# Gate rows of the forgetting attention: one load per pair, copied on ScalarE, triangle added on VectorE

## The chip, the cores and the metric

The kernel runs on one core of a Trainium2 chip. Its time is the device time of one execution in microseconds, and the time before is the median of three runs: 617.68 us (615.83, 617.68, 619.33).

## What is computed

The block normalises 512 tokens and 16 learned meta tokens ahead of them (L = 528, width 1024) and projects them with one combined weight into everything that follows. There are two attentions of 16 heads each: latent attention (MLA, with low-rank queries and keys and a rotary part) and forgetting attention (FoX, in the code's names `fox`). Both are causal; the second adds the cumulative log forget gate `cum` to its scores. Each output is gated by `silu` of a projection `z`, projected, mixed by two sigmoids, projected again, normalised and added to the input.

```
q (B,H,L,64), k, v:  s = q k^T * scale
fox only:            s = s + (cum[t] - cum[s])
s = where(key_pos <= query_pos, s, -inf);  p = softmax(s);  o = p v
y = (o * silu(z)) @ W_branch
h = h + rmsnorm_post((sigmoid(ga) * y_mla + sigmoid(gb) * y_fox) @ W_out)
```

In a row of the softmax the term `cum[t]` is the same for all keys and drops out, so that only the key's `cum[s]` has to be added: one row of 528 numbers for each head, the same for every query.

## The kernel before

**Stages.** A stage is one branch and one pair of heads, written (1,pr) for fox and (0,pr) for latent, pr = 0 to 7, in the order (1,0), (0,0), (1,1), (0,1) and so on. Each stage makes the scores of its pair for the four blocks of 128 queries (`s0` blocks 0 to 2, `s1` block 3), takes exponents on ScalarE (ACT; `e0`, `e1`), normalises them into probabilities `pn` in two float16 halves, high on ACT and low on VectorE (DVE; `n0`, `n1`), has the DMA engines transpose them into `pt`, and multiplies with the values (`va`, tile `ov`), which is done within the next stage.

**Fill.** Between these parts TensorE (PE) does the projections that later stages need, as a list of steps called `fill`. In a fox stage it is: 8 steps `za` (fox's own `z`), the transposes `vt` of the own values, `mq` (latent query), and then `mk` (latent keys, 2 steps), `v` (latent values, 2 steps) between the 8 steps of `zb` (the latent `z`). In a latent stage it is the next pair's `fq`, `vt`, `fk`, `v`. Products are three-pass: each operand stands as a high and a low part. A weight arrives as `wraw` by DMA, ACT casts its high part `wh`, and DVE or GpSimd (POOL) makes the remainder `wl` (helper at L117). Query and key go the same way into `hlq` and `hlk`: high part by ACT (L266), low part by DVE (L117), both from PSUM. The banks of these accumulators are few: the second key product takes the bank of `mq`, the first value product that of the first key product, so each waits until DVE has read the earlier one.

**The gate's rows.** `cdiag` [128, 2, 528] holds the two `cum` rows of a pair on all 128 partitions, loaded by `load_diag` (L285, two loads). `mask_diag` (L295) adds the causal triangle `maskt` to its four diagonal blocks. Blocks left of the diagonal need the rows without a triangle: `load_off` (L289) loads the first 400 numbers of each once more, into a free part of `gT`, two loads a pair. `terms` hands the scores the one or the other and L927 on DVE adds them as it reads the score from PSUM. Pair 0 is prepared at the start, where DVE adds the triangle; for pairs 1 to 7 POOL does.

**What sets the order.** Up to the end of stage (1,0) the order on all engines is written out by hand (lists of names, and the branch `si == 0`). In later stages only PE's order is by hand; on the other engines, SyncE (SP) with its DMA queue included, a scheduler places an instruction by its priority and by when its inputs and its buffer are free. So the rows of pair pr + 1 are loaded in stage (1,pr), once the scores of pair pr no longer read `cdiag`, though the code issues them with the keys in stage (0,pr). Each engine works its instructions in order, so an instruction that waits holds all behind it.

Of the kernel before, what the change touches and what calls it, by code (L numbers as in the profile page):

```python
# [17 lines left out]
ALU = mybir.AluOpType  # L18
# [8 lines left out]
NH = 16  # L27
KD = D // 128
# [26 lines left out]
def block_kernel(ctx: ExitStack, tc: tile.TileContext, x, meta_tokens, pre_norm_g, w_in, fox_forget_b,  # L55
                 mla_q_norm_g, mla_kv_norm_g, w_uq, w_ukv, w_br_mla, w_br_fox, w_out, post_norm_g,
                 rope_tok, rope_pe, out):
    nc = tc.nc
# [25 lines left out]
    c_dram = dram.tile([NH, L], F32, tag="cdram", name="c_dram")  # L84
# [16 lines left out]
    def total(cols):  # L101

        ps = acc(f"sum{uid[0]}")[:, 0:1]
        uid[0] += 1
        for i, c in enumerate(cols):
            mm(ps, ALL1, c, start=(i == 0), stop=(i == len(cols) - 1))
        return ps
# [85 lines left out]
    def unit(name, getw, act, nk, sls, done):  # L193

        st = {}
        out = []

        def make(eng=None, later=None):
            if "w" not in st:
                st["w"] = getw(eng, later) if eng else getw()  # L200
                loads = getattr(out[0][1], "nxt", ())
                if later is None:
                    for load in loads:
                        load()
                else:
                    later.extend(loads)

        for i, sl in enumerate(sls):
            n = sl.stop - sl.start
            for k in range(nk):  # L210
                def fn(i=i, sl=sl, k=k, n=n):
                    make()
                    if k == 0:
                        st["ps"] = acc(f"{name}{i}")
                    ps = st["ps"][:, :n]
                    (wh, wl), (ah, al) = st["w"], act(k)
                    for q, (w, a) in enumerate(((wh, ah), (wh, al), (wl, ah))):
                        mm(ps, w(k), a[:, sl], start=(k == 0 and q == 0), stop=(k == nk - 1 and q == 2))
                    if k == nk - 1:
                        done(i, ps)  # L220
                out.append((3 * n / 2.4, fn))
        out[0][1].make = make
        if hasattr(getw, "load"):
            out[0][1].load = getw.load
        return out
# [13 lines left out]
    def win_w(off, i):  # L239
        return weights(lambda: [win[:, :, off + 128 * i : off + 128 * i + 128]], lambda w: by_k(w[0], KD))  # L240

    def run(steps):
        for _, fn in steps:
            fn()
# [6 lines left out]
    cdiag = fx.tile([128, 2, L], F32, tag="cdiag", name="cdiag")  # L251
# [3 lines left out]
    def hl_done(key, n, w, put=None):  # L255

        def done(i, ps):
            if i == 0:
                hls[key] = hlp.tile([128, 2, n], F32R, tag=f"hl{key[0]}", name="hl" + "".join(map(str, key)))
            hl = hls[key]  # L260
            o = w * i
            w_ = min(w, n - o)

            def upper():
                with tc.high_priority(offset=30):
                    nc.scalar.copy(hl[:, 0, o : o + w_], ps)  # L266

            def lower():
                with tc.high_priority(offset=30):
                    split_lo(nc.vector, hl[:, 1, o : o + w_], ps, hl[:, 0, o : o + w_])  # L270
            if put:
                put(i, upper, lower)
            else:
                upper()
                lower()
        return done
# [4 lines left out]
    OFF = META + 384  # L281

    def load_diag(pr):
        for h in range(2):
            nc.sync.dma_start(cdiag[:, h], c_dram[2 * pr + h : 2 * pr + h + 1, :].broadcast_to([128, L]))  # L285

    def load_off(pr):
        for h in range(2):
            nc.sync.dma_start(gT[h][:, KD - 1, 0:OFF],  # L289
                              c_dram[2 * pr + h : 2 * pr + h + 1, 0:OFF].broadcast_to([128, OFF]))  # L290

    def mask_diag(eng):
        d = cdiag[:, :, META:].rearrange("p h (b c) -> p h b c", b=4)
        m = maskt[:, 400:L].unsqueeze(1).unsqueeze(1).broadcast_to([128, 2, 4, 128])
        eng.tensor_tensor(out=d, in0=d, in1=m, op=ALU.add)  # L295

    def k_fox(pr, put=None):
        halves = hl_done(("k", 1, pr), L, HALF, put)

        def done(i, ps):  # L300
            halves(i, ps)
            if pr > 1 and i:
                load_diag(pr)
                load_off(pr)
                mask_diag(nc.gpsimd)
        return unit(f"fk{pr}", win_w(O_FK, pr), u_act, KD, ALLT, done)


# [63 lines left out]
    def lo(name):  # L372

        def fn():
            for f in lows[name]:
                f()
        return fn
# [292 lines left out]
    with ExitStack() as att:  # L670
# [327 lines left out]
        vts = {}  # L998

        def feed(br, pr):  # L1000

            q = (q_mla, q_fox)[br](pr)
            k = (k_mla, k_fox)[br](pr)
            v, vts[br, pr] = v_unit(br, pr, put=(br, pr) == (0, 0))
            return q, k, v
# [8 lines left out]
        for si, (br, pr) in enumerate(stages):  # L1014
            last = si + 1 == len(stages)
            if not last:
                q, k, v = feed(*stages[si + 1])
            if br == 1:

                za, zb = z_unit(1, pr), z_unit(0, pr)  # L1020
                fill = za + vts[br, pr] + q + zb[:4] + k + zb[4:6] + v + zb[6:]
            elif not last:
                fill = q[:3] + vts[br, pr] + q[3:] + k + v
            else:
                g = gate_unit()
                g2 = gate_unit()

                def g_scale():
                    pow2_scale(sg[1], isg[1], total([gss[:, 1, c : c + 1] for c in range(4)]))
                fill = g[:4] + vts[br, pr] + g[4:] + g2[:4] + [(100, g_scale)] + g2[4:]  # L1030
            if si == 0:
                early = za[0][1], q[0][1], zb[0][1]
            fills.append(fill)
# [3 lines left out]
        za, q, zb = early  # L1037
# [10 lines left out]
        with tc.manual_schedule(engines={E_.PE, E_.SP, E_.Pool, E_.Activation, E_.DVE}):  # L1048
            for name in MIDDLE:
                later[name]()  # L1050
            lctx.close()
            gT = [gctx[b].enter_context(tc.tile_pool(name=f"gp{b}", bufs=1, side="right")).tile(
                [128, KD, S], F32, tag=f"gT{b}", name=f"gT{b}") for b in range(2)]
            later.update(r1=lambda: rope0[1](1), r0=lambda: rope0[1](0), Lf=fills[1][0][1].load,
                         Lo=lambda: load_off(0), bt=lambda: mask_diag(nc.vector))
            for name in LAST:
                later[name]()
        pe, pe_turn, pe_rest, _ = pe_unit(1)
# [5 lines left out]
        for si, (br, pr) in enumerate(stages):  # L1064
            (s0, e0), (s1, e1), n0, n1, va = attention(br, pr)

            fill = fills[si]
            with ExitStack() as head:
                if si == 0:
                    head.enter_context(tc.manual_schedule(engines={E_.PE, E_.SP, E_.Pool, E_.Activation, E_.DVE}))  # L1070
                    s0()
                    e0()
                    run(fill[:3])
                    lo("b")()
                    nxt[1].load()
                    nxt[2].load()
                    n0()
                    s1()
                    run(fill[3:9])
                    e1()  # L1080
                    run(fill[9:11])
                    n1()
                    load_diag(1)
                    load_off(1)
                    for x in (1, 0):
                        for i in range(2):
                            rope0[2](i, x, 2)
                    run(fill[11:17])
                    nxt[0].make()
                    run(fill[17:21])  # L1090
                    for name in ("vr0", "vr1", "vs", "vz"):
                        later[name]()
                    nxt[1].make()
                    run(fill[21:])
                    later["vT"]()
                    nxt[2].make()
                    mask_diag(nc.gpsimd)
                else:
                    s0()
                    e0()  # L1100
                    for fn in late:
                        fn()
                    s1()
                    e1()
                    run(fill[:4])
                    n0()
                    run(fill[4:11])
                    n1()
                    run(fill[11:])
            late = [va]  # L1110
# [281 lines left out]
    with rctx, ExitStack() as og:  # L1392
# [38 lines left out]
        for t in range(4):  # L1431
# [12 lines left out]
            for m in range(2):  # L1444
                sm = slice(512 * m, 512 * m + 512)
                nc.vector.scalar_tensor_tensor(out=yo[:, t, sm], in0=yo[:, t, sm], scalar=ss[:, t, 3:4],
                                               in1=xr[:, t, sm], op0=ALU.mult, op1=ALU.add)
# [44 lines left out]
```

## Time and profile before

| | us |
|---|---|
| median of three runs | 617.68 |
| profiled execution, its own time | 620.4 |
| its span | 618.4 |
| PE busy | 601.8 |
| DVE busy | 400.9 |
| ACT busy | 384.0 |
| POOL busy | 192.9 |
| first value product of (0,0) | 111.83 |

Rows of a timeline give start, duration, engine, line, operation, output and inputs, shape and count; in brackets stands the idle time before it and what ended that. Where a row counts several instructions, the duration is that of all. A row of windows gives, per engine in the order PE, PE's weight load, DVE, ACT, POOL, the busy time, then PE's granted clock as a share of the full one, the share of DMA and GB/s. A row of the waits view gives: engine, what waited, for what, us in total, times, longest. The shares of busy time are means over stages that differ.

### The profile page before, as it was taken

To read this page: it belongs to the slowest core of one execution; us is meant where nothing else is said; L and a number is where in the kernel's file an instruction comes from. 1 tells how busy PE (TensorE), PEld (TensorE's weight loads), DVE (VectorE), ACT (ScalarE), POOL (GpSimd) and SP (SyncE) were. 2 spreads that over 40 slices of the span, in tenths; PEclk is the share of its full clock that TensorE was granted. 3 is DMA by queue.
4 is the path that set the end of the run, shared out by engine and by line. 5 is a ranking of instruction groups with operands and counts; after the bars stand their busy time and mean duration, and the time that the engine had idled before them with its cause. 6 is when DMAs were issued, how large, how long until landed. Compare 5 with 4: busy or idle time off the path is not lost. (4 is left out here: it accounts for less than half of the span.)

```text
span 618.4 us, 11603 instructions
## 1 busy us (share of the span) xinstructions
PE 601.8 (97%) x3986; PEld 490.4 (79%) x3986; DVE 400.9 (65%) x1122; ACT 384.0 (62%) x839; POOL 192.9 (31%) x234
## 2 busy tenths in 40 slices
PE   8999999899999999999999999999999999999996
PEld 5889779689889889789888788787888865565885
DVE  5949874676765864874774775776977865556133
ACT  7756774675774874784794775776667654444421
POOL 2002572364672453544453553510000000003700
PEclk9999999899999999999999999999999999999999
DMA  9514667976896768576776965687252137333202
GB/s 301 132 36 138 170 174 186 206 184 157 236 178 156 165 167 176 132 178 163 179 169 156 178 156 141 142 161 231 61 151 75 35 94 246 103 107 98 102 35 102
DMA packets 209092, 92.12 MB, mean 149 GB/s; under 512 B 123113, under 2 KB 200297, under 8 KB 209034
## 3 DMA queue, kind: packets, MB, share of 16 engines
q1 hardware_dynamic: 209032, 91.39, 58.3%
q8 instruction: 31, 0.51, 0.3%
q14 instruction: 27, 0.22, 0.1%
q10 hardware_dynamic: 2, 0.00, 0.0%
HBM read 61.97 MB, written 3.97 MB: 107 GB/s over the span
## 5 line engine op out<-in xcount | busy, mean ns | idle before, releaser
L117 POOL TENSOR_TENSOR wl<-wraw,wh 128x1024 fp32r<-128x1024 f32 (+1 forms) x54 | 121.0, 2245 | 239.9 <-ACT wh L141 226.0
L141 ACT CAST wh<-wraw 128x1024 fp32r<-128x1024 f32 (+1 forms) x74 | 72.9, 987 | 82.7 <-issue 35.0
L937 ACT ACTIVATE sf<-sf,nb 128x272 f32<-128x272 f32 (+3 forms) x128 | 72.0, 567 | 16.7 <-DVE nb L927 16.6
L966 DVE SCALAR_TENSOR_TENSOR pn<-sf,ri,pn 128x128 f16<-128x128 f32 (+3 forms) x128 | 74.1, 619 | 2.9 <-ACT pn L965 2.5
L965 ACT ACTIVATE pn<-sf,ri 128x128 f16<-128x128 f32 (+3 forms) x128 | 61.8, 551 | 6.2 <-ACT sf L937 4.1
L91 PE MATMUL pg<-uTh,wh 128*128 128x512 f32 x128 | 51.9, 406 | 0.0
L91 PE MATMUL z<-uTh,wh 128*128 128x512 f32 x128 | 51.1, 399 | 0.0
L91 PE MATMUL z<-uTh,wl 128*128 128x512 f32 x128 | 50.1, 391 | 0.0
L91 PE MATMUL z<-uTl,wh 128*128 128x512 f32 x128 | 50.1, 391 | 0.0
L91 PE MATMUL pg<-uTh,wl 128*128 128x512 f32 x128 | 50.0, 391 | 0.0
L91 PE MATMUL pg<-uTl,wh 128*128 128x512 f32 x128 | 49.9, 390 | 0.0
L91 PE MATMUL st<-hlk,hlq 64*128 64x272 f32 (+3 forms) x480 | 46.8, 309 | 0.0
L91 PE MATMUL py<-g,yw 128*128 128x512 f16 x192 | 42.6, 379 | 0.6 <-DVE yw L1255 0.6
L91 PEld LDWEIGHTS st<-hlk,hlq 64*128 64x128 f32 x480 | 34.9, 185 | 7.0 <-ACT wh L141 2.9
L807 DVE TENSOR_REDUCE vsc<-v 128x1 f32<-128x272 f32 (+1 forms) x32 | 13.2, 432 | 36.5 <-PE v L91 36.5
L91 PE MATMUL fk<-uTh,wh 128*128 128x256 f32 (+1 forms) x128 | 36.6, 286 | 0.0
L91 PE MATMUL v<-uTh,wh 128*128 128x256 f32 (+1 forms) x128 | 36.5, 285 | 0.0
L91 PE MATMUL fk<-uTl,wh 128*128 128x256 f32 (+1 forms) x128 | 36.5, 285 | 0.0
L91 PE MATMUL fk<-uTh,wl 128*128 128x256 f32 (+1 forms) x128 | 36.5, 285 | 0.0
L91 PE MATMUL v<-uTl,wh 128*128 128x256 f32 (+1 forms) x128 | 36.4, 285 | 0.0
L91 PE MATMUL v<-uTh,wl 128*128 128x256 f32 (+1 forms) x128 | 36.4, 285 | 0.0
L91 PEld LDWEIGHTS <-yw 128*128 128x128 f16 x192 | 17.9, 98 | 22.7 <-DVE yw L1255 1.1
(303 smaller groups left out, 1547.4 us busy)
## 6 DMA issues: line engine op xcount, KB each, us to landing
wraw<-in_w_in_dram SPq DMA_DIRECT2D x56, 512.0 KB, 3.7
cdiag<-c_dram SPq DMA_DIRECT2D x16, 264.0 KB, 4.5
yraw<-in_w_br_fox_dram SPq DMA_DIRECT2D x8, 512.0 KB, 4.1
yraw<-in_w_br_mla_dram SPq DMA_DIRECT2D x8, 512.0 KB, 3.5
wraw<-in_w_out_dram SPq DMA_DIRECT2D x8, 512.0 KB, 3.5
gT<-c_dram SPq DMA_DIRECT2D x16, 200.0 KB, 4.8
pt<-pn SPq DMA_TRANSPOSE x128, 2.8
xr<-in_x_dram SPq DMA_DIRECT2D x4, 512.0 KB, 5.8
```

The lines of the kernel that those rows point to most:

```text
L91: nc.tensor.matmul(*a, **k)
L117: eng.tensor_tensor(out=lo, in0=src, in1=f32(hi), op=ALU.subtract)
L141: nc.scalar.copy(wh[:, :n], raw[:, :n])
L807: nc.vector.tensor_reduce(out=st["sc"][:, i : i + 1], in_=ps, op=ALU.max, axis=AX.X, apply_absolute_value=True)
L937: nc.scalar.activation(sf, sf, AF.Exp, bias=sums["nb"][:, h, b : b + 1], scale=-1.0, accum_out=sums["su"][:, h, b : b + 1])
L965: nc.scalar.activation(hi, sf, AF.Copy, scale=rib)
L966: nc.vector.scalar_tensor_tensor(out=lo, in0=sf, scalar=rib, in1=hi, op0=ALU.mult, op1=ALU.subtract)
```

## The change

`load_off` is gone. In its place `keep_off` has ACT copy the first 400 numbers of each row from `cdiag` into `gT`, before the triangle is added. The triangle is added by DVE for every pair. In the code `load_diag` for the next pair stands at the head of the latent stage, after its last exponents, and the copies and the triangle where the next pair's keys are done. In the fox stage's fill one more step of `zb` stands before `mk`, and one fewer after `v`. In stage (1,0), written by hand, the `vt` transposes come after `mq` rather than before, and the rest of the list is cut to match.

```diff
--- before.py
+++ after.py
@@ -284,25 +284,23 @@
         for h in range(2):
             nc.sync.dma_start(cdiag[:, h], c_dram[2 * pr + h : 2 * pr + h + 1, :].broadcast_to([128, L]))
 
-    def load_off(pr):
+    def keep_off():
         for h in range(2):
-            nc.sync.dma_start(gT[h][:, KD - 1, 0:OFF],
-                              c_dram[2 * pr + h : 2 * pr + h + 1, 0:OFF].broadcast_to([128, OFF]))
-
-    def mask_diag(eng):
+            nc.scalar.copy(gT[h][:, KD - 1, 0:OFF], cdiag[:, h, 0:OFF])
+
+    def mask_diag():
         d = cdiag[:, :, META:].rearrange("p h (b c) -> p h b c", b=4)
         m = maskt[:, 400:L].unsqueeze(1).unsqueeze(1).broadcast_to([128, 2, 4, 128])
-        eng.tensor_tensor(out=d, in0=d, in1=m, op=ALU.add)
+        nc.vector.tensor_tensor(out=d, in0=d, in1=m, op=ALU.add)
 
     def k_fox(pr, put=None):
         halves = hl_done(("k", 1, pr), L, HALF, put)
 
         def done(i, ps):
             halves(i, ps)
-            if pr > 1 and i:
-                load_diag(pr)
-                load_off(pr)
-                mask_diag(nc.gpsimd)
+            if pr and i:
+                keep_off()
+                mask_diag()
         return unit(f"fk{pr}", win_w(O_FK, pr), u_act, KD, ALLT, done)
 
 
@@ -1018,7 +1016,7 @@
             if br == 1:
 
                 za, zb = z_unit(1, pr), z_unit(0, pr)
-                fill = za + vts[br, pr] + q + zb[:4] + k + zb[4:6] + v + zb[6:]
+                fill = za + vts[br, pr] + q + zb[:5] + k + zb[5:7] + v + zb[7:]
             elif not last:
                 fill = q[:3] + vts[br, pr] + q[3:] + k + v
             else:
@@ -1052,7 +1050,7 @@
             gT = [gctx[b].enter_context(tc.tile_pool(name=f"gp{b}", bufs=1, side="right")).tile(
                 [128, KD, S], F32, tag=f"gT{b}", name=f"gT{b}") for b in range(2)]
             later.update(r1=lambda: rope0[1](1), r0=lambda: rope0[1](0), Lf=fills[1][0][1].load,
-                         Lo=lambda: load_off(0), bt=lambda: mask_diag(nc.vector))
+                         Lo=keep_off, bt=mask_diag)
             for name in LAST:
                 later[name]()
         pe, pe_turn, pe_rest, _ = pe_unit(1)
@@ -1076,25 +1074,23 @@
                     nxt[2].load()
                     n0()
                     s1()
-                    run(fill[3:9])
+                    run(fill[3:8])
                     e1()
                     run(fill[9:11])
+                    run(fill[8:9])
                     n1()
-                    load_diag(1)
-                    load_off(1)
                     for x in (1, 0):
                         for i in range(2):
                             rope0[2](i, x, 2)
-                    run(fill[11:17])
+                    run(fill[11:18])
                     nxt[0].make()
-                    run(fill[17:21])
+                    run(fill[18:22])
                     for name in ("vr0", "vr1", "vs", "vz"):
                         later[name]()
                     nxt[1].make()
-                    run(fill[21:])
+                    run(fill[22:])
                     later["vT"]()
                     nxt[2].make()
-                    mask_diag(nc.gpsimd)
                 else:
                     s0()
                     e0()
@@ -1102,6 +1098,8 @@
                         fn()
                     s1()
                     e1()
+                    if br == 0 and pr + 1 < NH // 2:
+                        load_diag(pr + 1)
                     run(fill[:4])
                     n0()
                     run(fill[4:11])
```

The order that follows, in three places (stage (1,1) on DVE and ACT, the queue of stage (1,0), and DVE at that stage's end). The names carry numbers of tiles; `pn_622` and `pn_623` are the probabilities of blocks 0 to 2 and of block 3.

DVE in the fox stage (1,1), from the last probability to the reductions on the latent values `v`; before:

```order
L863 TENSOR_TENSOR vm_629<-vm_1586,vm_629 16x128
L966 SCALAR_TENSOR_TENSOR pn_623<-sf_1495,ri_1427,pn_623 128x4x128
L117 TENSOR_TENSOR hlq_1604<-mq_1597,hlq_1604 128x512
L117 TENSOR_TENSOR hlk_1649<-mk_1645,hlk_1649 128x272
L117 TENSOR_TENSOR hlk_1649<-mk_1652,hlk_1649 128x256
L807 TENSOR_REDUCE vsc_1668<-v_1664 128x1
L807 TENSOR_REDUCE vsc_1668<-v_1670 128x1
```

and with the change:

```order
L861 TENSOR_TENSOR vm_629<-vm_1586,vm_629 16x128
L964 SCALAR_TENSOR_TENSOR pn_623<-sf_1495,ri_1427,pn_623 128x4x128
L117 TENSOR_TENSOR hlq_1604<-mq_1597,hlq_1604 128x512
L294 TENSOR_TENSOR cdiag<-cdiag,maskt 128x2x512
L117 TENSOR_TENSOR hlk_1652<-mk_1648,hlk_1652 128x272
L117 TENSOR_TENSOR hlk_1652<-mk_1655,hlk_1652 128x256
L805 TENSOR_REDUCE vsc_1671<-v_1667 128x1
L805 TENSOR_REDUCE vsc_1671<-v_1673 128x1
```

The triangle (`cdiag<-cdiag,maskt`) stands between the latent query's low half and the key's. It is the same in the fox stages (1,2) to (1,6). On POOL it stood before the remainder `wl` of the same stage and is gone. On ACT the two copies go in between `wh` and the keys' high halves:

```order
L266 CAST hlq_1604<-mq_1597 128x512
L141 CAST wh_1804<-wraw_1524 128x1024
L289 COPY gT_822<-cdiag 128x400
L289 COPY gT_826<-cdiag 128x400
L266 CAST hlk_1652<-mk_1648 128x272
L266 CAST hlk_1652<-mk_1655 128x256
L141 CAST wh_1875<-wraw_1595 128x1024
L870 ACTIVATE sil_1689<-z_1632 128x512
```

where before no row stood between `wh` and `hlk`, and the two casts `wh` that now stand further down followed each other behind `hlk`.

SP's queue round pair 1's rows, in stage (1,0); before:

```order
L973 DMA_TRANSPOSE pt_624<-pn_622 128x7x128
L973 DMA_TRANSPOSE pt_625<-pn_622 128x7x128
L973 DMA_TRANSPOSE pt_624<-pn_623 128x9x128
L973 DMA_TRANSPOSE pt_625<-pn_623 128x9x128
L285 DMA cdiag<-c_dram 128x528 x2
L289 DMA gT_822<-c_dram 128x400
L289 DMA gT_826<-c_dram 128x400
L786 DMA qpe_dram<-gT_822 6x16x512 x4
L132 DMA wraw_1069<-in_w_in_dram 128x8x128
```

and with the change:

```order
L971 DMA_TRANSPOSE pt_625<-pn_622 128x5x128
L971 DMA_TRANSPOSE pt_624<-pn_622 128x7x128
L971 DMA_TRANSPOSE pt_625<-pn_622 128x7x128
L285 DMA cdiag<-c_dram 128x528 x2
L971 DMA_TRANSPOSE pt_624<-pn_623 128x9x128
L971 DMA_TRANSPOSE pt_625<-pn_623 128x9x128
L784 DMA qpe_dram<-gT_822 6x16x512 x4
L132 DMA wraw_1068<-in_w_in_dram 128x8x128
L132 DMA wraw_1096<-in_w_uq_dram 128x2x64 x2
```

The two loads of `cdiag` come ahead of the last two of the eight transposes, those of `pn_623`; the loads of `gT` are gone. For pairs 2 to 7 the loads of `cdiag` keep their place: in the fox stage, behind the weight loads and ahead of the eight transposes.

DVE at the end of stage (1,0) and into (0,0), from the latent values' reductions to the first latent scores (`sf` read from `st`); with the change:

```order
L805 TENSOR_REDUCE vsc_1080<-v_1076 128x1
L805 TENSOR_REDUCE vsc_1080<-v_1081 128x1
L294 TENSOR_TENSOR cdiag<-cdiag,maskt 128x2x512
L810 TENSOR_SCALAR vsc_1080<-vsc_1080 128x1
L811 TENSOR_SCALAR vsc_1080<-vsc_1080 128x1
L813 TENSOR_SCALAR vsc_1080<-vsc_1080 128x1
L815 RECIPROCAL vsc_1080<-vsc_1080 128x1
L871 SCALAR_TENSOR_TENSOR sil_1104<-sil_1104,z_1035 128x512
L925 ISA sf_1120,nb_1117<-st_1121,maskt 128x144
L925 ISA nb_1117 128x1
```

Before, the rows are the same without the triangle. The triangle waits for ACT's two copies, which stand there behind one `wh` cast and ahead of another cast, `sil` (the latent `z`) and the exponents of (0,0).

## The prediction

> **What bounds the kernel now.** I read the page first, then TensorE's waits, then the timelines round each of those waits.
>
> ```profile
> span 618.4 us, 11603 instructions
> PE 601.8 (97%) x3986; PEld 490.4 (79%) x3986; DVE 400.9 (65%) x1122; ACT 384.0 (62%) x839; POOL 192.9 (31%) x234
> ...
> PE ov L91 <- DMA pt<-pn: 3.5, 4, 2.1
> PE mk L91 <- DVE hlq L117: 2.5, 3, 1.1
> PE vt L94 <- DVE nb L927: 1.8, 2, 1.0
> ...
> PE v L91 <- DVE hlk L117: 0.4, 1, 0.4
> ```
>
> TensorE (PE) is busy for 601.8 of 618.4 us and the change gives it no product more or less. So an edit counts only where it makes or ends a wait of PE, and the waits that it can end come to 3.5 + 2.5 + 1.8 + 0.4 = 8.2 us. The mask, the rows and the copies lie on other engines; what I need from each is when it ends, and which PE row waits for that.
>
> The 2.5 us of `mk` waits are the triangle's. The clearest of them, in fox stage (1,4):
>
> ```profile
> 258.49 2.15 POOL L295 TENSOR_TENSOR cdiag<-cdiag,maskt 128x1024 f32<-128x1024 f32 x1 [3.34 <-DMA cdiag<-c_dram]
> ...
> 258.49 2.70 DVE L966 SCALAR_TENSOR_TENSOR pn<-sf,ri,pn 128x512 f16<-128x512 f32 x1
> 261.11 0.68 DVE L117 TENSOR_TENSOR hlq<-mq,hlq 128x512 fp32r<-128x512 f32 x1
> ...
> 260.16 0.29 PE L91 MATMUL mk<-cTh,wh 128*128 128x272 f32 x1
> 261.84 0.39 PE L91 MATMUL mk<-cTh,wh 128*128 128x256 f32 x1 [1.13 <-DVE hlq L117]
> 263.69 0.29 PE L91 MATMUL v<-cTh,wh 128*128 128x272 f32 x1
> ...
> 79.42 1.42 DVE L966 SCALAR_TENSOR_TENSOR pn<-sf,ri,pn 128x512 f16<-128x512 f32 x2 [0.85 <-ACT pn L965]
> ```
>
> GpSimd (POOL) and VectorE (DVE) start at 258.49 together. The `pn` operation, 0.71 us each in the pair at 79.42, takes 2.70: it runs only once POOL's 2.15 us are over. The query's low half (`hlq`) is late behind it, and the second key product, which takes the query's PSUM bank, waits 1.13 us. From the first key product to the first value product it is 3.53 us; undisturbed, in stage (1,5), it is 307.08 - 304.95 = 2.13 (rows below). So 1.40 is lost, 0.27 more than the wait that the view shows.
>
> **The change part by part.**
>
> *The triangle leaves POOL in the six fox stages (1,1) to (1,6).* The three `mk` waits of 2.5 us, each 0.27 more from start to start, and a fourth stage with about 0.3 in the same measure, are gone: -3.6. I take it whole, since no other POOL operation lies ahead of `pn` and `hlq` there.
>
> *The triangle comes to DVE, between the query's low half and the key's.* ScalarE's (ACT) two copies stand before it, after the weight cast `wh`. Stage (1,5), which has no loss now:
>
> ```profile
> 303.45 1.05 ACT L141 CAST wh<-wraw 128x1024 fp32r<-128x1024 f32 x1
> ...
> 304.58 2.41 POOL L117 TENSOR_TENSOR wl<-wraw,wh 128x1024 fp32r<-128x1024 f32 x1 [0.74 <-ACT wh L141]
> ...
> 304.32 0.68 DVE L117 TENSOR_TENSOR hlq<-mq,hlq 128x512 fp32r<-128x512 f32 x1
> 305.95 0.77 DVE L117 TENSOR_TENSOR hlk<-mk,hlk 128x272 fp32r<-128x272 f32 x2 [0.96 <-ACT hlk L266]
> ...
> 304.95 0.29 PE L91 MATMUL mk<-cTh,wh 128*128 128x272 f32 x1
> 305.69 0.39 PE L91 MATMUL z<-uTh,wh 128*128 128x512 f32 x1
> 307.08 0.29 PE L91 MATMUL v<-cTh,wh 128*128 128x272 f32 x1
> ...
> L937 ACT ACTIVATE sf<-sf,nb 128x400 f32<-128x400 f32 x32 | 19.7, 618 | 0.0
> ```
>
> The copies have no row of their own. Nearest is ACT's operation on 128x400 at 0.62; two of them behind the cast that ends at 304.50 end by 305.7, and hide in ACT's pause before the key's upper half. At the same 304.50 the cast also releases POOL's weight remainder `wl`, which runs to 306.99. So the triangle always arrives at DVE while POOL is in `wl`. What that means the head of the first stages shows, the one place where the triangle is on DVE already:
>
> ```profile
> 59.97 1.24 DVE L117 TENSOR_TENSOR wl<-wraw,wh 128x1024 fp32r<-128x1024 f32 x1
> 61.45 1.99 DVE L295 TENSOR_TENSOR cdiag<-cdiag,maskt 128x1024 f32<-128x1024 f32 x1 [0.24 <-DMA cdiag<-c_dram]
> ...
> 60.13 4.45 POOL L771 TENSOR_TENSOR pt<-pt 128x512 f32<-128x512 f32 x2
> 64.55 2.54 POOL L117 TENSOR_TENSOR gT<-pt,gT 128x512 fp32r<-128x512 f32 x2
> ```
>
> POOL's operations on 128x512 take 1.27 each in the last row. The pair at 60.13 takes 4.45: the first stands until DVE's `wl` ends at 61.21 and runs to about 62.4, the triangle stands until then and ends at 63.44, after about 1.1 of its own, and POOL's second starts after it. The two take turns by whole operations. `hlq` and `hlk` read PSUM and aren't held (0.68 and 0.77 for two, during `wl`).
>
> Hence in (1,5): the triangle stands until 306.99, ends at 308.09, the first `hlk` (0.36) at 308.45, and the first value product, which takes the key's PSUM bank, starts at about 308.5. PE is there at 307.08 + 0.69 = 307.77, since the changed order puts one more step of `z` ahead of it (two steps take 307.08 - 305.69). The stall is 0.73. The same working gives 0.61 to 0.71 in the other five: together +4.1. If the triangle were not held it would end at 306.8 and `hlk` at 307.2, in time: bound 0. If `wl` itself took 2.84, as in stage (1,4) behind POOL's triangle, each stall would be 0.43 longer: bound +6.7. I take 4.1, because both pairings in these rows show the turn-taking.
>
> By the Trainium skill, page "SBUF — State Buffer", section "SBUF: two separate sides", VectorE and GpSimd share a port pair that whichever starts first holds for its whole instruction, a VectorE operation with two SBUF inputs counting against a GpSimd operation that reads SBUF. By that rule six triangles stand behind six `wl`, and the rows agree (2.70 against 0.71); it speaks against the change in these stages.
>
> *DMA.* The 16 loads of 200 KB are gone, 3.2 of 92 MB. In the six stages the transposes that PE waits for start when `pn` is written, later than these loads, so I take 0, bounded by the small `ov` waits of those stages: -0.4 for the one in (1,5), whose transposes have the later `z` arrival as cover (a PE that is 0.7 late no longer waits there). I take -0.4.
>
> *The first two stages, (1,0) and (0,0).* These rows carry them:
>
> ```profile
> 71.84 11.93 SPq L973 DMA_TRANSPOSE pt<-pn  x8
> 83.82 1.05 SPq L285 DMA_DIRECT2D cdiag<-c_dram  x2
> ...
> cdiag<-c_dram SPq DMA_DIRECT2D x16, 264.0 KB, 4.5
> ...
> 82.19 1.05 ACT L141 CAST wh<-wraw 128x1024 fp32r<-128x1024 f32 x1 [0.71 <-issue]
> 83.66 0.60 ACT L872 ACTIVATE sil<-z 128x512 f32<-128x512 f32 x1 [0.41 <-PE z L91]
> ...
> 85.15 0.31 DVE L927 CUSTOM_DVE_ANT_0 sf<-st,maskt 128x144 f32<-128x144 f32 x1 [0.17 <-PE st L91]
> ...
> 92.41 0.66 PE L94 MATMUL vt<-ident,vT 128*128 128x128 f32 x4 [0.85 <-DVE nb L927]
> 108.22 1.52 PE L91 MATMUL st<-hlk,hlq 64*128 64x144 f32 x18
> 112.93 0.58 PE L91 MATMUL ov<-pt,vm 80*64 80x512 f16 x1 [0.72 <-DMA pt<-pn]
> 117.10 0.50 PE L91 MATMUL z<-uTh,wh 128*128 128x512 f32 x1
> ...
> 86.08 1.80 PE L91 MATMUL ov<-pt,vp 128*64 128x512 f16 x24
> 112.94 3.31 PE L91 MATMUL ov<-pt,vp 128*64 128x512 f16 x24
> ...
> 108.80:112.20 3.40, 1.31 (x13) 0.82 (x12) 3.30 (x23) 3.09 (x12) 2.53 (x2) 1.00 1.11 244
> 112.20:115.60 3.40, 2.68 (x17) 1.74 (x17) 0.17 (x2) 1.28 (x5) 0.00 (x0) 0.50 1.01 288
> ```
>
> Moving the value transposes behind `mq` saves the first `vt` wait of 1.0 and puts `hlk` some 0.8 later on DVE: about 0 when the first latent scores begin (83.6 both ways). But pair 1's rows, now loaded between the sixth and the seventh transpose, issue at about 83.8 - 2 x 11.93/8 = 80.8 and land, at 4.5 and one issue apart, by 86.3. ACT's copies wait for that and end at 86.9, the cast behind them at 87.9, and `sil`, which began at 83.66, at 88.4. DVE has its triangle (86.9 to 88.0), the four small `vsc` operations and `sil` behind it, so the first latent score is read at 89.4 instead of 85.15. PE has other products for part of it; its `vt`, which already waits 0.85 for DVE, comes at about 95.9 instead of 92.41: +3.5.
>
> That delay then meets a stall that is there already. PE arrived at the values of (0,0) at 108.22 + 1.52 = 109.74, waited 2.09 and 0.72, started at 112.93, and ran at half clock in the window from 112.20 (0.50): the 24 products of 1.80 took 3.31, 1.5 more. Its transposes are issued at times that SP's queue sets, so I let them stand at 112.5 or before. PE now arrives at 113.2, does not wait, and has no idle stretch behind it. The next `z` follows at 113.2 + 0.2 (a first product, which now stands before 112.93) + (117.10 - 112.94) - 1.5 = 116.1, against 117.10: -1.0. With rows that land in 3.2 us (the fastest of the 16 loads, against 4.5) the delay is 1.3 less: -2.3, if the transposes are ready by then. With 6.0 (the slowest) and the half clock as now it is -1.0 + 1.5 + 1.5 = +2.0.
>
> On that clock, the Trainium skill, page "TensorE: Matmul & The Clock Gate", section "What's actually happening", has it halve after an idle window of about 3.4 us. The window here was 3.40 with 1.31 busy, so the trace shows it halved for less; by the page new stalls of 0.7 cost no clock, and by the trace they would only if some 2 us of them came together.
>
> *Sum:* -3.6 + 4.1 - 0.4 - 1.0 = -0.9. The profiled execution took 620.4 (span 618.4); it would be 619.5. The median of the runs shown is 617.68, 2.7 lower, and there the same change gives 616.8.
>
> **The rivals.**
>
> *The triangle is not held* (or `hlk` comes in time some other way, since the changed placing of `wl` on POOL isn't known to the tenth): the 4.1 falls away, so -5.0, and 612.7. For it speaks that the stall hangs on `wl` starting at the very moment the copies do; against it, that all operations of this kind in the rows take turns.
>
> *The head loses, slower.* The mechanism: ACT and DVE stand in order behind the landing of pair 1's rows; if the `pn` operations behind them also make the last transposes of (0,0) late, the 3.5 is added on top of the old stall rather than taking its place. It decides from transposes that land after 113.2: then +3.5 with the steady part at 0.1, 621.3. Against it: SP's queue, not `pn`, set these transposes before (they follow weight loads that end at 97).
>
> *The stalls are longer than worked out:* `wl` at 2.84 gives +2.6 over the six, 619.4, and a half-clock stretch 1.5 more, 620.9.
>
> *It does not do what it says:* in the changed order the loads of pairs 2 to 7 stay where they were, in the fox stage's queue ahead of its transposes, not at the head of the latent stage. So that is certain, and priced: those rows land as before and nothing moves by it.
>
> **How the numbers follow.** Chances: forecast 0.50, triangle not held 0.22, head slower 0.14, longer stalls 0.14. A measurement of this kernel can tell about 0.5% (3.1 us) from no change. The forecast's own range is 614 to 620.5, by the bounds of the head (-2.3 to +2.0) and 1 us each way on the sum of the six stalls: 0.08 of it below 614.6, 0.03 above 620.8. Not held is faster but for 0.02; head slower is slower but for 0.03; longer stalls are slower in 0.09 of 0.14. So faster 0.28, same 0.49, slower 0.23. The range of 8 in 10 reaches to 612.5, just past the case that isn't held, and to 621.5, past the other two. The likeliest is 616.8.
>
> **What would show it.** Right: no `mk` wait on `hlq` in the waits, in its place six `v` waits on `hlk` of 0.6 to 0.75; each triangle on DVE at about 1.1 plus the rest of a `wl`, 2.5 or more as the profile counts it; an ACT copy in stage (1,0) that waits for `cdiag`, the first latent score read at about 89.4; no wait at the values of (0,0) and no window at 0.50 there. Wrong: `v` waits missing or near 1.2; the values of (0,0) still waiting for transposes after an arrival at 113; a new half-clock window; or a wait in a latent stage, which I have none for.

## The result

The changed kernel takes 621.56 us (median of 7 runs, 620.49 to 621.74) against 618.66 us for the kernel before (7 runs, 615.83 to 620.25): ratio 1.005, 95% interval 1.0029 to 1.0072. Forecast were 616.8 and "no change"; it is slower. Two later timings of the same two kernels gave 1.0036 (1.0019 to 1.0053) and 1.0015 (1.0000 to 1.0031), differences of the medians of 2.4 and 1.4 us; the last interval just reaches 1. Over the three timings together, 63 runs of the kernel before have a median of 619.71 and 31 of the changed kernel 621.56. So the loss is real but small, 1 to 3 us, and runs of the kernel before scatter over more than that.

The page and TensorE's (PE's) waits of the changed kernel:

```profile
span 619.9 us, 11591 instructions
PE 603.1 (97%) x3986; PEld 490.9 (79%) x3986; DVE 408.9 (66%) x1129; ACT 389.0 (63%) x855; POOL 176.5 (28%) x227
...
PE ov L91 <- DMA pt<-pn: 5.0, 4, 3.2
PE v L91 <- DVE hlk L117: 4.1, 7, 1.0
```

The `mk` waits on `hlq` (2.5 us) and the `vt` waits on `nb` (1.8) are gone. In their place `v` waits seven times for `hlk`: once for 1.0 in stage (1,0), and about 0.5 in each of the six fox stages. The `ov` waits for transposes grew from 3.5 to 5.0, and the longest of them is in another stage.

One of the six, stage (1,5), timeline of the changed kernel:

```profile
304.23 1.05 ACT L141 CAST wh<-wraw 128x1024 fp32r<-128x1024 f32 x1
305.18 0.95 ACT L289 COPY gT<-cdiag 128x400 f32<-128x400 f32 x2
...
305.36 2.40 POOL L117 TENSOR_TENSOR wl<-wraw,wh 128x1024 fp32r<-128x1024 f32 x1 [4.61 <-ACT wh L141]
...
306.17 2.68 DVE L294 TENSOR_TENSOR cdiag<-cdiag,maskt 128x1024 f32<-128x1024 f32 x1 [0.74 <-ACT gT L289]
308.77 0.76 DVE L117 TENSOR_TENSOR hlk<-mk,hlk 128x272 fp32r<-128x272 f32 x2
...
309.25 0.40 PE L91 MATMUL v<-cTh,wh 128*128 128x272 f32 x1 [0.53 <-DVE hlk L117]
309.48 0.28 PE L91 MATMUL v<-cTl,wh 128*128 128x272 f32 x1
309.60 0.29 PE L91 MATMUL v<-cTh,wl 128*128 128x272 f32 x1
```

The copies took 0.5 us each and hid. The triangle was issued to VectorE (DVE) at 306.17 and ended at 308.85, 1.09 after GpSimd's (POOL's) `wl` ended at 307.76: it stood through the rest of `wl`, as forecast. `hlk` and the value product followed. One thing was not forecast: the product that waited is followed by the next after 0.23 us, where the one behind that follows after 0.12. So a wait costs PE 0.27 us more than its row says (0.80 in place of 0.53, by the table below): 0.11 by this slower first product, and 0.16 because the row counts from the end of the product ahead, while a product that doesn't wait starts before that end (0.23 after the start of a product of 0.39).

The head, stage (1,0) into (0,0), changed kernel:

```profile
71.84 9.32 SPq L971 DMA_TRANSPOSE pt<-pn  x6
81.26 1.01 SPq L285 DMA_DIRECT2D cdiag<-c_dram  x2
82.37 4.86 SPq L971 DMA_TRANSPOSE pt<-pn  x2
...
86.44 0.52 ACT L289 COPY gT<-cdiag 128x400 f32<-128x400 f32 x1 [5.08 <-DMA cdiag<-c_dram]
...
87.67 1.22 DVE L294 TENSOR_TENSOR cdiag<-cdiag,maskt 128x1024 f32<-128x1024 f32 x1 [5.09 <-ACT gT L289]
...
90.10 0.30 DVE L925 CUSTOM_DVE_ANT_0 sf<-st,maskt 128x144 f32<-128x144 f32 x1
...
88.27 0.38 PE L91 MATMUL ov<-pt,vm 80*64 80x512 f16 x1 [3.17 <-DMA pt<-pn]
89.26 0.38 PE L91 MATMUL ov<-pt,vm 80*64 80x512 f16 x1 [0.61 <-DMA pt<-pn]
...
96.53 0.66 PE L94 MATMUL vt<-ident,vT 128*128 128x128 f32 x4
```

The two loads stand ahead of the last two transposes. These now take 4.86 to issue, 3.47 of it the last one, where all eight took 11.93 before and the last one 1.32. PE, which ran its values at 85.84 without a wait in the kernel before, gets them at 88.27 and 89.26. Meanwhile ScalarE (ACT) and DVE stand behind the landing for 5 us each.

The windows of the changed kernel there, and at the values of (0,0):

```profile
83.35:86.77 3.42, 1.75 (x24) 1.52 (x23) 0.00 (x0) 0.33 (x1) 0.47 (x1) 1.00 0.77 179
86.77:90.18 3.41, 1.30 (x11) 0.73 (x12) 2.40 (x7) 2.71 (x6) 0.69 (x2) 1.00 0.83 168
90.18:93.59 3.41, 3.41 (x31) 3.02 (x29) 2.17 (x12) 3.41 (x11) 3.41 (x2) 0.50 0.62 180
110.80:114.20 3.40, 3.40 (x36) 2.87 (x36) 1.60 (x10) 1.50 (x3) 0.68 (x1) 1.00 0.92 203
114.20:117.60 3.40, 3.40 (x40) 2.55 (x35) 3.40 (x22) 3.40 (x14) 1.87 (x2) 1.00 1.05 276
```

The old stall at 110 to 113 is gone, and so is the half clock behind it, as forecast. But both are back one stage earlier: PE busy 1.75 and 1.30 of 3.4, then a clock of 0.50.

To place the loss, I divided the profiled executions at PE's own rows, for every kernel profiled here. Head is the time to the first `vt` of stage (1,1). "Keys and values" is the sum over the six fox stages of the way from their `vt` to the next `ov`, which holds the `mk` and `v` waits. "To the next vt" is the way on from there, which holds the `ov` waits. All in us.

| kernel | head | keys and values | to the next vt | own time |
|---|---|---|---|---|
| before, first profile | 122.7 | 71.6 | 34.7 | 620.4 |
| before, second profile | 123.4 | 71.3 | 34.2 | 619.5 |
| before, loads early | 122.4 | 70.3 | 35.4 | 619.2 |
| changed, first | 122.7 | 72.6 | 35.4 | 621.7 |
| changed, second | 123.1 | 72.6 | 35.0 | 621.7 |
| changed, third | 123.2 | 72.6 | 35.0 | 621.2 |
| changed, pair 1's load last | 126.3 | 72.5 | 33.8 | 623.4 |
| changed, pair 1 as before (two profiles) | 123.9, 123.1 | 72.4, 72.4 | 33.8, 34.0 | 621.2, 619.9 |
| changed, pair 1 on ACT's queue | 121.2 | 72.5 | 36.1 | 621.8 |
| changed, triangle behind hlk | 122.8 | 68.0 | 36.7 | 618.1 |
| changed, triangle on POOL behind wl | 123.2 | 67.8 | 35.3 | 617.0 |
| triangle behind hlk, pair 1 as before | 120.8 | 67.9 | 35.3 | 614.1 |
| triangle behind hlk, pair 1 on ACT's queue | 120.0 | 68.3 | 35.9 | 615.7 |

Each row is one execution, and the own time shows which: "pair 1's load last" and "pair 1 on ACT's queue" were profiled in the slowest of their 12 runs, the last two kernels in the fastest of theirs. These last two are also the only profiles in which PE's clock is never halved in the head, though their first two stages have the same code as the rows "pair 1 as before" and "pair 1 on ACT's queue". So heads of single profiles differ by 1 to 3 us for the same code.

The rest of the span lies between 388.5 and 390.2 us for all. Undisturbed, keys and values take 11.31 a stage, 67.9. The kernel before loses 3.7, 3.4 and 2.4 there, 3.2 in the mean; the seven profiles with the changed place of the triangle lose 4.6 to 4.7. That is +1.5, and it is the one difference between the two kernels that stands clear of the scatter.

### The profile page after: what moved, and what is told of

Its sections match the earlier page's. It is cut to its first block, busy times and chain, and to the rows that moved or that the text cites. A ratio compares the mean times of both kernels' runs of the same rounds, so it can differ in the third digit from the quotient of the medians.

```text
span 619.9 us, 11591 instructions
## 1 busy us (share of the span) xinstructions
PE 603.1 (97%) x3986; PEld 490.9 (79%) x3986; DVE 408.9 (66%) x1129; ACT 389.0 (63%) x855; POOL 176.5 (28%) x227
## 5 line engine op out<-in xcount | busy, mean ns | idle before, releaser
L117 POOL TENSOR_TENSOR wl<-wraw,wh 128x1024 fp32r<-128x1024 f32 (+1 forms) x54 | 119.4, 2214 | 276.1 <-ACT wh L141 264.2
L964 DVE SCALAR_TENSOR_TENSOR pn<-sf,ri,pn 128x128 f16<-128x128 f32 (+3 forms) x128 | 65.8, 554 | 2.9 <-ACT pn L963 2.5
```

What stands on the lines that cost most here:

```text
L117: eng.tensor_tensor(out=lo, in0=src, in1=f32(hi), op=ALU.subtract)
L964: nc.vector.scalar_tensor_tensor(out=lo, in0=sf, scalar=rib, in1=hi, op0=ALU.mult, op1=ALU.subtract)
```

## The experiments

The twelve runs below came in three groups, each with its own runs of the kernel before; its median was 620.88, 619.65 and 619.79 us in them, against 618.66 in the first timing. So ratios are compared across groups, and medians within one.

### The triangle's place on DVE

*Behind `hlk`.* In each fox stage the triangle is queued behind the two low halves of the latent key, whose instructions are kept in `lows`; only the order of issue is set, no wait is added:

```diff
-                mask_diag()
+                with tc.issue_after(lows["k", 0, pr - 1].ins):
+                    mask_diag()
```

> The changed kernel with one edit: in every fox stage the triangle on VectorE is queued behind the two low halves of the latent key (hlk), not ahead of them. Theory A (the triangle stands behind GpSimd's weight remainder and hlk stands behind the triangle): the six v waits on hlk of (1,1) to (1,6) go, 6 x (0.69 + 0.11 of a slower first product) = 4.8 us, so 621.6 - 4.8 = 616.8. Rival B (the waits come from the new order of the z and key steps, or from the copies on ScalarE): the v waits stay and the time stays at 621.5. Stage (1,0) is untouched: its wait of 3.2 at the values stays under both.

Measured 618.19 us, 0.9962 of the kernel before (0.9946 to 0.9978), and a profile of 618.1 against 621.7. Its rows for stage (1,5) and the wait that is left at one of the later values:

```profile
303.88 2.41 POOL L117 TENSOR_TENSOR wl<-wraw,wh 128x1024 fp32r<-128x1024 f32 x1 [4.62 <-ACT wh L141]
...
305.93 0.77 DVE L271 TENSOR_TENSOR hlk<-mk,hlk 128x272 fp32r<-128x272 f32 x2 [1.99 <-ACT hlk L267]
306.62 1.22 DVE L296 TENSOR_TENSOR cdiag<-cdiag,maskt 128x1024 f32<-128x1024 f32 x1
...
307.05 0.29 PE L91 MATMUL v<-cTh,wh 128*128 128x272 f32 x1
...
180.89 0.38 PE L91 MATMUL ov<-pt,vm 80*64 80x512 f16 x1 [0.72 <-DMA pt<-pn]
```

`hlk` runs inside `wl` without being held, the triangle begins after `wl` and takes 1.22, and no `v` product waits in the six stages. Theory A holds, B falls. The size is less sure: from the changed kernel's 1.0015 to 1.005 down to 0.9962 it is 3.3 to 5.4 us, and by the profiles 3.6 and not 4.8, since PE arrives earlier at the next values and waits for transposes there (the column to the next `vt` is 36.7 against 35.0 to 35.4).

*On POOL, behind `wl`.* The copies stay on ACT; pairs 2 to 7 get their triangle on POOL, which now waits for the copies and so stands behind `wl` instead of ahead of it:

```diff
-                mask_diag()
+                mask_diag(nc.gpsimd if pr > 1 else nc.vector)
```

> The changed kernel with the triangle of pairs 2 to 7 on GpSimd again; there it now stands behind the weight remainder wl, because it waits for ScalarE's copies; copies, z order and pair 1 as changed. Theory A (the six v waits come from the triangle on VectorE standing behind wl): no v wait and no mk wait in the six stages, since pn is done before GpSimd begins the triangle; 3.6 us below the changed kernel, about 0.998 of the kernel before. Rival B (the v waits come from the copies or the z order): they stay.

Measured 617.26 us, 0.9962 (0.9939 to 0.9986), 3.9 below the changed kernel of the same group. Its POOL rows in stage (1,5):

```profile
303.17 2.40 POOL L117 TENSOR_TENSOR wl<-wraw,wh 128x1024 fp32r<-128x1024 f32 x1 [4.62 <-ACT wh L141]
305.54 2.15 POOL L294 TENSOR_TENSOR cdiag<-cdiag,maskt 128x1024 f32<-128x1024 f32 x1
```

Keys and values take 67.8 there, as if undisturbed. So the copies and the new order of the steps cost nothing in the six stages, and the engine is not the point either. What matters is which two operations meet: ahead of `wl` the triangle meets `pn`, on DVE ahead of `hlk` it meets `wl`, and in these two kernels it meets nothing that PE waits for.

### Pair 1 and the first two stages

*The loads behind the eighth transpose.*

```diff
                     n1()
+                    load_diag(1)
```

> The changed kernel with one edit: pair 1's two gate-row loads are issued behind the eighth transpose of stage (1,0) instead of ahead of the seventh. Theory A (the loads delay the last two transposes): the wait of 3.2 + 0.6 at the values of (1,0) goes. But ScalarE's copies and VectorE's triangle still stand in order behind the landing, now at about 89, so the first latent score is read at about 92.5 instead of 90.1 and TensorE waits later, at vt; net between -1.5 and +1.5: 620 to 623. Rival B (only the transposes matter, the blocked ScalarE and VectorE are covered): 621.6 - 3.8 = 617.8.

Measured 622.0 us, 1.0027 (1.0011 to 1.0042); the head is 126.3, some 3.3 longer than that of the changed kernel. PE's waits:

```profile
PE st L91 <- DVE nb L925: 5.0, 1, 5.0
PE v L91 <- DVE hlk L117: 4.1, 7, 1.0
```

The wait for transposes at the values is gone, as theory A has it. The other half of the forecast mechanism then shows alone: DVE, behind the copies and the landing, keeps PE's next scores for 5.0 us. In this profile that costs more than the wait it replaces, and behind it PE's clock is halved for 6.83 us from 93.20. By the medians it doesn't: 1.0027 lies among the changed kernel's 1.0015 to 1.0050, and 622.0 within the 620 to 623 of theory A. Rival B's 617.8 falls. So later loads are not shown to be better or worse, only not to win back the wait.

*Pair 1 prepared as before*: loads behind the eighth transpose, two more loads for the rows without triangle, triangle on POOL. It was timed in two groups.

```diff
                     n1()
+                    load_diag(1)
+                    load_off(1)
 ...
                     nxt[2].make()
+                    mask_diag(nc.gpsimd)
 ...
-            if pr and i:
+            if pr > 1 and i:
```

> The changed kernel with pair 1 prepared as in the kernel before: its loads behind the eighth transpose, two more loads for the rows without triangle, the triangle on GpSimd; pairs 2 to 7 as changed. It shares the loss out. Theory A (head and six stages both lose, the six stages about 1.2 to 1.6): 618.7 + 1.4 = 620.1. Rival B (the whole loss is in the first two stages): 618.7. Rival C (the whole loss is in the six stages): 621.5.

> The changed kernel with pair 1 prepared as before (loads behind the eighth transpose, two more loads, triangle on GpSimd), now beside the changed kernel itself. Theory A (by the medians the larger part of the loss is in the first two stages): 1.5 to 2.5 us below the changed kernel, within 1 us of the kernel before. Rival B (the loss is in the six stages, as the pairs of profiles had it): within 0.7 us of the changed kernel.

Measured 620.6 us, 1.0008 (0.9991 to 1.0024), and 620.2 us, 1.0005 (0.9986 to 1.0024). In the second group the changed kernel stood beside it:

> The changed kernel, timed beside the three other runs of this group as their yardstick. Expected 1.0035 to 1.005 of the kernel before, with the waits of 3.2 + 0.6 at the values of (1,0) and six v waits of 0.5.

621.15 us, 1.0015. The difference is 0.95 us, and the intervals overlap. Theory A of the second text asked for 1.5 to 2.5, rival B for less than 0.7; neither is shown. The two profiles put the head of this kernel at 123.9 and 123.1, no shorter than the changed kernel's. The changed kernel itself came out below the 1.0035 to 1.005 expected of it; its waits at `v` were there again (4.1 in seven), and its first wait at the values of (1,0) was 2.76.

*The loads early in the kernel before*, and nothing else:

```diff
+                    load_diag(1)
                     n1()
-                    load_diag(1)
                     load_off(1)
```

> The kernel before with one edit: pair 1's two cdiag loads ahead of the seventh transpose of stage (1,0), as in the changed kernel; the gT loads, GpSimd's triangle and all else as before, so that neither ScalarE nor VectorE waits for the landing. Theory A (the loads push the last two transposes back): a wait of 3 to 4 at the values of (1,0). At the values of (0,0), where the kernel before waits 2.8 for its own transposes and then runs at half clock, TensorE then comes later and waits up to 2.8 less: net 0 to +2. Rival B (the transposes come late only because ScalarE or VectorE is blocked): no wait at the values of (1,0), net 0.

Measured 619.19 us, 0.9983 (0.9964 to 1.0001). SyncE's queue and PE's first two value products:

```profile
71.93 9.11 SPq L973 DMA_TRANSPOSE pt<-pn  x6
81.14 1.00 SPq L285 DMA_DIRECT2D cdiag<-c_dram  x2
82.24 4.79 SPq L973 DMA_TRANSPOSE pt<-pn  x2
...
88.19 0.38 PE L91 MATMUL ov<-pt,vm 80*64 80x512 f16 x1 [2.28 <-DMA pt<-pn]
89.16 0.40 PE L91 MATMUL ov<-pt,vm 80*64 80x512 f16 x1 [0.59 <-DMA pt<-pn]
96.30 0.60 PE L94 MATMUL vt<-ident,vT 128*128 128x128 f32 x4
```

Here neither ACT nor DVE waits for the landing, and the picture is the changed kernel's: the same 4.8 us for the last two transposes, a wait at the values, `vt` at 96.30. So the place in the queue makes this wait, as theory A says (2.28 and 0.59, a little under the 3 to 4 expected), and it alone makes `vt` late. It costs nothing in the end, because the stall at the values of (0,0) and the half clock behind it are gone in return (head 122.4).

*The loads on ACT's own queue*, behind the exponents of block 3, with the copies and the triangle kept behind the same neighbours as in the changed kernel (for pair 1 they are queued behind the latent key's halves):

```diff
                     e1()
+                    load_diag(1, nc.scalar)
```

> The changed kernel with one edit: pair 1's two loads are issued by ScalarE on its own queue, behind the exponents of block 3 of stage (1,0), at about 76.5, so that the transposes on SyncE's queue aren't moved; the copies stay behind the same weight cast and the triangle behind the same reductions. Theory A (the head's loss is the place in the queue: it delays the last two transposes and the landing): rows land by 82, the wait of 3.8 at the values of (1,0) is at most 0.3, the first latent score is read by 86.5 instead of 90.1, and the time falls by 2.5 to 4: 617.6 to 619 on the scale of the first timing (621.6), so about 0.999 of the kernel before. Rival B (the loads slow the transposes wherever they are issued, by sharing the DMA engines): the wait stays above 2 us and the time within 1 of the changed kernel.

Measured 619.0 us, 0.9991 (0.9974 to 1.0008), 3.0 below the changed kernel of its group (622.02, 1.0036). Rows:

```profile
76.87 0.35 ACTq L287 DMA_DIRECT2D cdiag<-c_dram  x1
78.05 0.33 ACTq L287 DMA_DIRECT2D cdiag<-c_dram  x1
...
73.62 12.11 SPq L976 DMA_TRANSPOSE pt<-pn  x8
...
83.82 0.96 ACT L291 COPY gT<-cdiag 128x400 f32<-128x400 f32 x2
...
83.68 0.39 PE L91 MATMUL v<-cTh,wh 128*128 128x272 f32 x1 [1.79 <-DVE hlk L271]
```

The transposes issue in 12.11 as in the kernel before, the values do not wait, and the copies do not wait for a landing. Theory A holds on the queue, and rival B falls. But the first latent score is read at 88.68, where A wanted 86.5 and the changed kernel has 90.10. The gain is not the 3.8 of that wait: `hlq` on ACT comes later behind the issuing, at 78.42, and `v` waits 1.8 instead of 1.0. The 3.0 us rest on the medians alone; the profiled execution took 621.8, with half clock from 84.24 behind that wait at `v`.

### Both repairs, and the same kernels again

The triangle behind `hlk` with pair 1 as before, and with pair 1's loads on ACT's queue:

> The edits of the runs with the triangle behind hlk and with pair 1 prepared as before, together: the copies on ScalarE and the triangle on VectorE kept for pairs 2 to 7. Theory A: no triangle wait on TensorE in the six stages, neither mk nor v: 620.1 - 4.8 = 615.3, below the kernel before by the 3.4 us that its own mk waits cost. Rival B (a later wait takes their place, for instance the transposes at the values): 617 to 619.

> Both repairs of the changed kernel: pair 1's loads on ScalarE's queue, and the triangle behind the low halves of the latent key. Theory A: the two losses add up, so this is 3.6 below the run with pair 1's loads on ScalarE's queue alone (what the six v waits were worth by the profiles), about 0.993 of the kernel before. Rival B: waits for the transposes take part of it, 0.996 or above.

Measured 617.01 us, 0.995 (0.9931 to 0.9968), and 616.0 us, 0.9933 (0.9913 to 0.9953). No product waits for the triangle in the six stages of either. The first is 3.9 below the kernel before of its group by the medians and 3.1 by the ratio, where theory A wanted 3.4; that its 617.01 falls into rival B's span comes from that group's slower runs of the kernel before. The second is 3.0 below the run with the loads on ACT's queue alone by the medians and 3.6 by the ratios, where 3.6 was expected, and 3.65 below the kernel before of its group. Its ratio is the lowest of all, but the two intervals overlap. It keeps what the change was made of, copies instead of loads and the triangle on DVE, and differs in the place of two things. Waits for transposes take a part back in the first (35.3 to the next `vt`, against 33.8 and 34.0 without its edit); in the second they don't (35.9 against 36.1).

The changed kernel and the kernel before once more:

> The changed kernel as it stands, timed beside the other runs of this group and profiled once more. Expected 1.003 to 1.007 of the kernel before. Theory A (the loss is in the first two stages and the six stages vary by the transposes): the waits of 3.2 + 0.6 at the values of (1,0) and the six v waits of 0.5 are there again, while the waits of 0.3 to 0.8 at the later values come at other places or not at all. Rival B (the six stages lose 1.5 us each time): the part from the first vt of (1,1) to the end is again 1.5 longer than in the first profile of the kernel before.

> The kernel before, profiled once more. Theory A (its first two stages vary from run to run by the wait for the transposes at the values of (0,0) and the half clock behind it): the first vt of (1,1) starts between 119 and 124, not at 122.7 again, while the way from there to the end stays within 1 us of the first profile. Rival B: both are within 0.5 us of the first profile.

The changed kernel gave 622.02 us, 1.0036, with the same waits at the values of (1,0) (3.19 and 0.63) and at `v`. The way from the first `vt` of (1,1) to the end was 496.8 against 495.7 in the first profile of the kernel before, 1.1 longer where rival B wanted 1.5. The wait at the values of (1,5) came at the same place (0.86), where A wanted other places or none. The kernel before has its first `vt` of (1,1) at 123.4, inside the span that A gave, but the way from there to the end was 1.7 shorter than in the first profile. So the picture of a head that varies and a steady rest is not borne out: in the kernel before both vary, by 0.7 and 1.7 us.

## Why the prediction was wrong

Its mechanisms were nearly all seen. Its sum was -0.9, and the medians say +1.4 to +2.9. Term by term:

- *The triangle's stalls on DVE, +4.1.* Right in mechanism, and in size as far as it was worked out: in the six stages of seven profiles every triangle ends 1.07 to 1.09 after its `wl`, and the first `v` products of the changed kernel start 4.1 late in all, as forecast. (The rows show 0.44 to 0.55 and not the 0.6 to 0.75 of the forecast, since they count from the end of the product ahead.) Yet keys and values lose 4.6 to 4.7 in the seven profiles. The 0.6 that was missing is the slower first product behind each wait, 6 x 0.11. I had counted it in the stalls that go (1.40 from start to start where the row says 1.13) and left it out of those that come.
- *The triangle's stalls on POOL, -3.6.* Taken from one execution. Three executions of that part, one of them of the kernel with the loads early, lost 3.7, 3.4 and 2.4; the mean is 3.2. What one profile shows of a stall that hangs on when a load lands is one draw. The stalls that come hang on `wh`, `wl` and the triangle alone, and vary by 0.1.
- *The small `ov` wait, -0.4.* Not seen. In (1,5) it is 0.80 in the changed kernel against 0.41. That column scatters by 1 us either way with the same code.
- *The head, -1.0.* This is the step that failed. The forecast priced the early loads for the engines that wait for the rows (ACT's copies, DVE's triangle, the first latent score at 89.4: seen at 90.10; `vt` at 95.9: seen at 96.53). It did not price them for what they were moved past. In the row of eight transposes, which the forecast itself quoted, two were to be issued behind two loads, and PE waits for the last of them. The `vt` came at about the time forecast, but by coincidence, and PE's row says why: it had stood 3.17 and 0.61 at the values, and the kernel with early loads and no wait on ACT or DVE has it at the same time. The gain at the values of (0,0) came as forecast, no wait and full clock. The wait and the half clock of (1,0) took it back, and a new half-clock window was among the forecast's own signs of being wrong. In time the two delays overlap, so the next `z` came 1.0 later than forecast (117.08 for 116.1): 0.6 by the later `vt`, and 0.4 because the way from the values to `z` takes 3.27 undisturbed, where 2.9 was worked out. The head was 122.7 and 123.4 in two profiles before and 122.7, 123.1 and 123.2 in three of the changed kernel: 0 in place of -1.0.

With these corrections the sum is -0.9 + 0.6 + 0.4 + 0.4 + 1.0 = +1.5. That lies within the three timings, at their lower end; together they have 1.85. The corrections are read from the profiles, whose own times differ by 1.6 in the mean (619.9 before, 621.5 changed), so they show where the profiled loss lies and are no second measurement of it.

Of the rivals, "head loses" named a late head, but by another way: it had the transposes of (0,0) late, and these were in time. "Not held" is refuted by all seven profiles with the changed place of the triangle. "Longer stalls" wanted a longer `wl`, which ran at 2.39 to 2.41 each time in these seven.

What stays open is some tenths of a microsecond up to 1. The first timing has 2.9, the first pair of profiles 1.3 in own time. With pair 1 as before the median is 0.95 us nearer to the kernel before in the group that timed both, while the profiles show no shorter head for it. The waits for the transposes move by 1 us between executions of one kernel. A single profile in each group can't tell where the medians differ.

## What to carry to other kernels

When a transfer is moved in a queue, price it first for what it now stands ahead of, and only then for who waits for it. When an operation moves between two engines that take turns, ask which operation it will meet: the same triangle cost 3.2 us ahead of `wl` on POOL, 4.6 ahead of `hlk` on DVE, and none behind either. A stall that hangs on the landing of a load should be sized from several executions before it is booked as a gain.

## What was not expected of the hardware

- Two plain loads ahead of two transposes in one queue cost the transposes more than their own 1.0 us of issuing: the last transpose alone took 3.47 to issue instead of 1.32 (3.33 to 3.57 in five profiles with this order), and the values came 2.4 us later, 88.27 against 85.84. Why the last one takes so long is not shown.
- The granted clock can halve behind a stretch in which PE was not idle. In every profile its changes in the first 600 us lie whole multiples of 3.41 us apart, so PE's busy time can be counted in the clock's own steps, as in the first three windows shown for the head. In the changed kernel the step from 83.35 with 1.75 us busy kept the clock, the one from 86.77 with 1.30 lost it. Over the fourteen profiles, twelve steps at full clock were busy for at most 1.62 us, and each was followed by half clock; none with 1.68 or more was. So in these traces it turns on about half of a step. The Trainium skill, page "TensorE: Matmul & The Clock Gate", section "What's actually happening", speaks of an idle window; here eleven of the twelve had 0.38 us of work or more in them.
- The first product after a wait of PE is followed 0.23 us later by the next, where 0.12 is usual at this shape, so each short wait has a cost that its own row does not show.
